# A rotation kernel: three output buffers and 63 chunks in place of two and 68, with the last load emitted later

## Chip, cores, metric

One core of a Trainium2 chip; the other cores are idle. The metric is the device time of the slowest core in microseconds (us), as the median of several runs. The span of a profile is about 1.8 us shorter than the time of the same run.

## The reference

`np.rot90(x, 1)` of an 8192 x 8192 float32 matrix: 268 MB are read and 268 MB written.

```python
def reference(x, k):            # k = 1
    return np.rot90(x, k)
```

## The kernel before

The matrix is worked through in macro tiles of 1024 rows x 4096 columns. The last one is cut into two of 512 rows, the "last macro tile but one" and the "last". Each macro tile has eight loads (2 MiB each, issued by SP, the sync engine, into an input buffer `a`), 64 chunks (DVE, the vector engine, copies 128 x 512 pieces with columns reversed into `ar`), and eight outputs. For an output, PE, the tensor engine, transposes 32 blocks into two tiles of PSUM, the memory that it writes to; ACT, the scalar engine, evicts (copies) each into an output buffer `ot`, and ACT issues the store (2 MiB). "The tail" is the work on the last two, smaller macro tiles. A load may be issued when all eight copies out of its buffer are done, and the buffer is that of the load two before. A store's buffer comes free when the store has landed.

```python
    a_pool = ctx.enter_context(tc.tile_pool(name="a_pool", bufs=2))
    r_pool = ctx.enter_context(tc.tile_pool(name="r_pool", bufs=68))
    o_pool = ctx.enter_context(tc.tile_pool(name="o_pool", bufs=2))
    psum_pool = ...                                   # bufs=2
    def load(r0, rt, c0):
        for t in range(rt):
            if loads < RT and loads % 4 >= 2:
                a = o_pool.tile([P, W], dt, tag="o")  # first eight loads only
            else:
                a = a_pool.tile([P, W], dt, tag="a")
            nc.sync.dma_start(out=a[:], in_=x[...])
            for j in range(W // CH):                  # 8 chunks a load
                ar = r_pool.tile([P, CH // P, P], dt, tag="ar")
                nc.vector.tensor_copy(out=ar[:], in_=a[...][:, :, ::-1])
                chunks[t, j] = ar
    def store(r0, rt, c0, chunks, end, first):
        for i, g0 in enumerate(range(0, W // P, G)):
            if end and (i + first) % 2 == 0:
                ot = a_pool.tile([P, F], dt, tag="a") # in the tail: input buffers too
            else:
                ot = o_pool.tile([P, F], dt, tag="o")
            for h in range(0, G, PW):
                pt = psum_pool.tile(...)
                for w in range(PW):
                    for t in range(rt):
                        nc.tensor.transpose(ps[...], chunks[t, ...][...], ident)
                nc.scalar.copy(o[...], ps)
                ...                                   # and, per output, the store:
                nc.scalar.dma_start(out=dst, in_=o[...])
    for m in most:
        store(*m, load(*m), False, 0)
    c1 = load(*before_last)
    c2 = load(*last)
    store(*before_last, c1, True, 1)
    store(*last, c2, True, 1)
```

Of the kernel before, what the change touches and what calls it, by code (L numbers as in the profile page):

```python
# [2 lines left out]

# [5 lines left out]

P = 128  # L10




R = 1024
RT = R // P
LAST = [4, 4]
W = 4096
CH = 512
F = 4096  # L20
FP = 2048


def whole_reads(nc):






    for fn in nc.m.functions:
        for block in fn.blocks:
            for n, ins in enumerate(block.instructions):
                if not isinstance(ins, mybir.InstDMACopy):
                    continue
                src = ins.ins[0]
                ap = [list(d) for d in src.ap]
                if len(ap) == 3 and ap[2][0] == 1 and ap[1][0] == ap[2][1]:
                    ap = [ap[0], [1, 1], [1, ap[1][1] * ap[2][1]]]
                    block.instructions[n] = copy.replace(  # L40
                        ins,
                        ins=[copy.replace(src, ap=ap)],
                        ant_dge_precooked=False,
                    )


def macro_tiles(N, M):

    tiles = [(r0, RT, c0) for r0 in range(0, N, R) for c0 in range(0, M, W)]
    r0, _, c0 = tiles.pop()  # L50
    for n in LAST:
        tiles.append((r0, n, c0))
        r0 += n * P
    return tiles


@with_exitstack
def kernel(
    ctx: ExitStack,
    tc: tile.TileContext,  # L60
    x: bass.AP,
    k: bass.AP,
    out: bass.AP,
):
    nc = tc.nc
    assert k == 1, f"only k=1 supported, got {k}"
    nc.at_finalize(whole_reads)

    N, M = x.shape
    dt = x.dtype  # L70

    consts = ctx.enter_context(tc.tile_pool(name="consts", bufs=1))
    ident = consts.tile([P, P], dt)
    make_identity(nc, ident)

    a_pool = ctx.enter_context(tc.tile_pool(name="a_pool", bufs=2))
    r_pool = ctx.enter_context(tc.tile_pool(name="r_pool", bufs=68))
    o_pool = ctx.enter_context(tc.tile_pool(name="o_pool", bufs=2))
    psum_pool = ctx.enter_context(
        tc.tile_pool(name="psum", bufs=2, space=bass.MemoryType.PSUM)  # L80
    )

    loads = 0

    def load(r0, rt, c0):





        nonlocal loads
        chunks = {}
        for t in range(rt):


            if loads < RT and loads % 4 >= 2:
                a = o_pool.tile([P, W], dt, tag="o")
            else:
                a = a_pool.tile([P, W], dt, tag="a")
            loads += 1  # L100
            nc.sync.dma_start(  # L101
                out=a[:], in_=x[r0 + t * P : r0 + (t + 1) * P, c0 : c0 + W]
            )
            for j in range(W // CH):
                ar = r_pool.tile([P, CH // P, P], dt, tag="ar")
                nc.vector.tensor_copy(  # L106
                    out=ar[:],
                    in_=a[:, j * CH : (j + 1) * CH].rearrange(
                        "r (b m) -> r b m", m=P
                    )[:, :, ::-1],  # L110
                )
                chunks[t, j] = ar
        return chunks

    def store(r0, rt, c0, chunks, end, first):





        rows = rt * P
        PW = 1
        while 2 * PW * rows <= FP:
            PW *= 2
        G = PW
        while 2 * G * rows <= F:
            G *= 2
        for i, g0 in enumerate(range(0, W // P, G)):
            if end and (i + first) % 2 == 0:
                ot = a_pool.tile([P, F], dt, tag="a")  # L130
            else:
                ot = o_pool.tile([P, F], dt, tag="o")
            o = ot[:, : G * rows].rearrange("m (g f) -> m g f", g=G)

            S = PW if end and r0 + rows == N and g0 + G == W // P else G
            for h in range(0, G, PW):
                pt = psum_pool.tile([P, FP], mybir.dt.float32, tag="ps")
                ps = pt[:, : PW * rows].rearrange("m (g f) -> m g f", g=PW)
                for w in range(PW):
                    g = g0 + h + w  # L140
                    for t in range(rt):
                        nc.tensor.transpose(  # L142
                            ps[:, PW - 1 - w, t * P : (t + 1) * P],
                            chunks[t, g * P // CH][:, g % (CH // P), :],
                            ident,
                        )
                nc.scalar.copy(o[:, G - PW - h : G - h, :], ps)  # L147

                done = h + PW
                if done % S == 0:  # L150
                    top = M - c0 - (g0 + done) * P
                    dst = out[top : top + S * P, r0 : r0 + rows].rearrange(
                        "(g m) f -> m g f", g=S
                    )
                    nc.scalar.dma_start(  # L155
                        out=dst, in_=o[:, G - done : G - done + S, :]
                    )

    tiles = macro_tiles(N, M)
    *most, before_last, last = tiles  # L160
    for m in most:
        store(*m, load(*m), False, 0)

    c1 = load(*before_last)
    c2 = load(*last)
    store(*before_last, c1, True, 1)
    store(*last, c2, True, 1)


# [1 line left out]
_INS = ['x', 'k']  # L171
_OUTS = [((8192, 8192), 'float32')]

_NUMBERS = {'k': 1}


# [26 lines left out]
```

## Time and profile before

Time before: 1269.7 us median (1269.53 to 1270.23). The page of the profile gives the busy times and the span in 40 slices. The DMA row is the mean busy share of the 16 DMA engines in tenths, the row below it what they moved. The last line here is the chain that ended last, by line.

```profile
span 1267.9 us, 10385 instructions
PE 708.5 (56%) x4096; PEld 668.7 (53%) x4096; DVE 355.1 (28%) x1024; ACT 467.6 (37%) x257; POOL 0.7 (0%) x6
...
DMA  9999999999999999999999999999999999999989
GB/s 399 418 430 429 430 429 429 430 428 430 428 429 429 429 428 429 429 430 429 428 430 429 429 427 425 424 429 429 429 429 423 417 426 427 428 429 429 429 361 374
...
q8 instruction: 32, 0.52, 0.2%
...
DMA out_dram<-ot 73%; ACT ot L147 19%; DMA a<-in_x_dram 4%; PE pt L142 1%; DVE ar L106 0%; ACTq L155 0%; SPq L101 0%; ACTq L147 0%; DVEq L106 0%
```

No compute engine is busy for more than 56%. The DMA row stands at 9 nearly throughout at about 429 GB/s. The Trainium skill ("Perfetto Trace Analysis", section Roofline) says that a single active core is bounded by its 16 DMA engines at about 435 GB/s together; the 429 of this trace agrees. The two weak slices at the end, 361 and 374, are what the change goes for. The windows of 5 us show them closer; the last two columns are the DMA share and GB/s.

```profile
core 0: us, PE busy (x) PEld busy (x) DVE busy (x) ACT busy (x) POOL busy (x), PEclk, DMA share, GB/s
1210.00:1215.00 5.00, 1.35 (x7) 1.36 (x8) 0.80 (x3) 3.27 (x2) 0.00 (x0) 0.87 0.83 349
1215.00:1220.00 5.00, 4.03 (x27) 3.78 (x25) 2.11 (x7) 0.56 (x2) 0.00 (x0) 0.79 0.82 347
1220.00:1225.00 5.00, 3.28 (x30) 3.24 (x31) 0.67 (x2) 4.25 (x3) 0.00 (x0) 1.00 0.43 180
1225.00:1230.00 5.00, 4.19 (x37) 3.67 (x34) 0.00 (x0) 4.33 (x3) 0.00 (x0) 1.00 1.00 416
1260.00:1265.00 5.00, 0.00 (x0) 0.00 (x0) 0.00 (x0) 0.00 (x0) 0.00 (x0) 0.50 0.94 388
```

Between 1210 and 1225 us the engines carry little: a hole worth 4.8 us of mean DMA time (the sum of (429 - rate)/429 x 5 us over the three windows). ACT's timeline shows where it comes from:

```profile
1205.54 0.55 ACTq L155 DMA_DIRECT2D out_dram<-ot  x1
1211.73 3.63 ACT L147 COPY ot<-pt 128x2048 f32<-128x2048 f32 x2 [6.22 <-DMA out_dram<-ot]
1215.39 0.55 ACTq L155 DMA_DIRECT2D out_dram<-ot  x1
1219.80 3.63 ACT L147 COPY ot<-pt 128x2048 f32<-128x2048 f32 x2 [4.44 <-DMA out_dram<-ot]
1223.47 0.55 ACTq L155 DMA_DIRECT2D out_dram<-ot  x1
```

With two output buffers, the eviction at 1219.80 waited (4.44 us idle) for the store issued at 1205.54. Its own store is issued only at 1223.47, when little is left in the queues.

Two more views are needed later: what SP's load issues waited for, and what the engines waited for in total (columns: total us, times, longest us).

```profile
SPq L101 <- DMA a<-in_x_dram: 798.5, 124, 12.3
SPq L101 <- DVE ar L106: 353.3, 124, 3.2
```

One view is not in the page: the 16 semaphore updates that each transfer leaves in the trace, one for each DMA engine. The Trainium skill ("DMA: Bandwidth & Descriptors", section "Why a DMA increments its semaphore by 16 and not by 1") says that the engines of one DMA finish independently and that only the full 16 means that the data has landed. The trace agrees: the 16 updates of the first load lie within 0.4 us, those of the load landing at 1217.8 spread over 8.9 us. "The slowest engine" below is the last of these 16; the kept records don't number the engines, so it need not be the same engine each time. There are 257 transfers (128 loads, 129 stores, the last output being two halves); the slowest engine's 247th lands at 1219.7, its last at 1267.0.

### The profile page before, as it was taken

How to read it: one execution, taken by the hardware profiler on the slowest of the kernel's cores; microseconds unless marked ns; L12 is line 12 of the kernel's file. 1: busy time of each engine (PE TensorE's matmuls, PEld its weight loads, DVE VectorE, ACT ScalarE, POOL GpSimd, SP SyncE). 2: the span in 40 equal slices, each digit the busy share in tenths (PEclk: the TensorE clock that was granted, in tenths of full speed). 3: DMA queues.
4: the chain of work that ended last, by engine and by line, in shares of the span. 5: the costliest groups of instructions: out<-in, count | busy, mean ns of one | idle time of the engine just before them, and what ended most of it. 6: DMA issues, size and time to landing. Idle time of an engine off the chain costs nothing.

```text
span 1267.9 us, 10385 instructions
## 1 busy us (share of the span) xinstructions
PE 708.5 (56%) x4096; PEld 668.7 (53%) x4096; DVE 355.1 (28%) x1024; ACT 467.6 (37%) x257; POOL 0.7 (0%) x6
## 2 busy tenths in 40 slices
PE   1456555655655556555556556565564655656674
PEld 0356455654655545554555545464564654645663
DVE  4422322232223322232223222232222322232210
ACT  0333344333433343333433334333433334333454
POOL 0000000000000000000000000000000000000000
PEclk9976767677677776776778767778777677677697
DMA  9999999999999999999999999999999999999989
GB/s 399 418 430 429 430 429 429 430 428 430 428 429 429 429 428 429 429 430 429 428 430 429 429 427 425 424 429 429 429 429 423 417 426 427 428 429 429 429 361 374
DMA packets 37057, 537.55 MB, mean 424 GB/s; under 512 B 4112, under 2 KB 4112, under 8 KB 4112
## 3 DMA queue, kind: packets, MB, share of 16 engines
q10 hardware_dynamic: 18576, 268.44, 49.9%
q1 hardware_dynamic: 18432, 268.44, 49.8%
q8 instruction: 32, 0.52, 0.2%
q14 instruction: 17, 0.14, 0.0%
HBM read 268.44 MB, written 268.44 MB: 423 GB/s over the span
## 4 chain that ended last, share of the span: by engine, by line
DMA 77%; ACT 19%; PE 1%; issue 1%; DVE 0%; ACTq 0%; SPq 0%; DVEq 0%
DMA out_dram<-ot 73%; ACT ot L147 19%; DMA a<-in_x_dram 4%; PE pt L142 1%; DVE ar L106 0%; ACTq L155 0%; SPq L101 0%; ACTq L147 0%; DVEq L106 0%
## 5 line engine op out<-in xcount | busy, mean ns | idle before, releaser
L142 PE MATMUL pt<-ident,ar 128*128 128x128 f32 x4096 | 708.5, 353 | 542.9 <-ACT ot L147 462.9
L142 PEld LDWEIGHTS pt<-ident,ar 128*128 128x128 f32 x4096 | 668.7, 189 | 582.4 <-ACT ot L147 493.5
L147 ACT COPY ot<-pt 128x2048 f32<-128x2048 f32 x256 | 466.3, 1869 | 745.1 <-DMA out_dram<-ot 732.6
L106 DVE COPY ar<-a 128x512 f32<-128x512 f32 x1024 | 355.1, 421 | 865.6 <-DMA a<-in_x_dram 781.4
L147 ACT ACT_TABLE_LOAD x1 | 1.3, 1283 | 41.0 <-DVE ar L106 41.0
masks.py:199 POOL TENSOR_SCALAR_AFFINE_SELECT ident<-ident 128x128 f32<-128x128 f32 x1 | 0.3, 294 | 0.1
masks.py:197 POOL MEMSET ident<- 128x128 f32 x1 | 0.2, 205 | 0.3 <-POOLq L184 0.3
L184 POOL MEMSET const-uint8-127<- 128x1 uint8 x1 | 0.1, 103 | 0.0
L184 POOL MEMSET const-bfloat16-1.0<- 128x1 bf16 x1 | 0.1, 102 | 0.0
L184 POOL MEMSET const-float32-0.0<- 128x1 f32 x1 | 0.1, 99 | 0.2 <-issue 0.2
L184 POOL MEMSET const-float32-1.0<- 128x1 f32 x1 | 0.1, 99 | 0.0
## 6 DMA issues: line engine op xcount, KB each, us to landing
a<-in_x_dram SPq DMA_DIRECT2D x128, 2048.0 KB, 16.8
out_dram<-ot ACTq DMA_DIRECT2D x127, 2048.0 KB, 15.8
out_dram<-ot ACTq DMA_DIRECT2D x2, 1024.0 KB, 12.9
```

The costliest lines, as they stand in the source:

```text
L106: nc.vector.tensor_copy(out=ar[:], in_=a[:, j * CH : (j + 1) * CH].rearrange("r (b m) -> r b m", m=P)[:, :, ::-1],)
L142: nc.tensor.transpose(ps[:, PW - 1 - w, t * P : (t + 1) * P], chunks[t, g * P // CH][:, g % (CH // P), :], ident,)
L147: nc.scalar.copy(o[:, G - PW - h : G - h, :], ps)
L184: nc = _bacc.Bacc("TRN2", target_bir_lowering=False, num_devices=1)
```

## The change

The intent: with a third output buffer, an output's eviction waits for the store three before instead of two before, so that in the tail stores are issued in time and the hole is filled. The space comes from the chunks, 63 instead of 68. That is one fewer than a macro tile has, and in the tail 32 + 32 chunks are loaded before an output frees any, so the last load must be emitted behind the first output, or the program would wait for itself.

```diff
-    r_pool = ctx.enter_context(tc.tile_pool(name="r_pool", bufs=68))
-    o_pool = ctx.enter_context(tc.tile_pool(name="o_pool", bufs=2))
+    r_pool = ctx.enter_context(tc.tile_pool(name="r_pool", bufs=63))
+    o_pool = ctx.enter_context(tc.tile_pool(name="o_pool", bufs=3))
...
-            if loads < RT and loads % 4 >= 2:
+            if loads < RT and loads % 5 >= 2:
...
-        return chunks
+            yield chunks
...
-            if end and (i + first) % 2 == 0:
+            if end and i % 2:
...
-    c1 = load(*before_last)
-    c2 = load(*last)
-    store(*before_last, c1, True, 1)
-    store(*last, c2, True, 1)
+    *_, chunks = load(*before_last)
+    outputs = store(*before_last, chunks, True)
+    rows = load(*last)
+    for _ in range(last[1] - 1):
+        next(rows)
+    next(outputs)
+    chunks = next(rows)
+    for _ in outputs:
+        pass
+    for _ in store(*last, chunks, True):
+        pass
```

No engine's order of instructions changes; only waits do.

## The prediction

> What bounds it. The page's slices show the DMA engines at 90% or more nearly throughout, at about 429 GB/s; PE is busy 56%, ACT 37%, DVE 28%. The chain of waits is 73% stores. 537 MB at 429.8 GB/s take 1251 us of the 1267.9 us span. The other 17 us, by windows of 20 us: 2.9 in the first 60 us, about 5 spread over the middle (dips near 740-820 and 960-1020), 9.1 after 1200 us, of which 2.9 is the final drain.
>
> The tail hole. Windows of 5 us: 349 GB/s at 1210-1215, 347 at 1215-1220, 180 at 1220-1225, then about 417 while only stores run. Against 429 that is 4.8 us. Its cause in the timeline: with two output buffers, output k's eviction waits for store k-2. The first output of the last macro tile but one waits until 1219.8 for the store issued at 1205.5, evicts for 3.6 us, and is stored from 1223.5, when the queue is all but dry. From then on ACT issues a store each 4.3 us, faster than the 4.9 to 5.0 us that 2 MiB take.
>
> What the change does. No transfer, copy, transpose or eviction is added or removed. Output k waits for store k-3. In the tail that first output can be evicted at about 1211.7 and stored from 1215.4, the next (into an input buffer, free at 1210.8) from 1219.7: both parts of the hole should be filled. The price: 63 chunks are one fewer than a macro tile's 64, so each tile's last copy waits for its first output's transposes (by the built program: the next load is issued about 6 us after the eighth lands, not 3). Loads take 16.8 us from issue to landing, so about 10 us of work still stand in the queues; I expect no cost. The last load's new place only prevents a deadlock: its own wait is unchanged, so it lands at 1218 as before. The start is equal within 0.6 us.
>
> How much is critical: not all 4.8 us. A DMA counts 16 engines that finish independently (the Trainium skill, "DMA: Bandwidth & Descriptors", section on why a DMA increments its semaphore by 16). The trace agrees: the 16 landings of one load spread over 0.4 us at the start, 8.9 us at 1217. The slowest engine lands at 1219.7, 1224.7, 1230.2 to 1230.8: it sat idle only 0.5 to 1.1 us in the hole, where the fast ones waited and all came level. Then one engine falls 1.9 us behind (a 16 KB instruction fetch at 1230.3) and sets the end, 1267.0. Without the hole the slowest engine goes on at 5.0 us a store: 1219.7 + 9 x 4.97 = 1264.5, or 1266.4 if a late fetch hits it. So the gain is 0.6 to 2.5 us, up to 4.8 if skew doesn't carry through. I predict 1267.3 us, range 1264.8 to 1269.7; faster by over 2% 0.01, within 2% 0.98, slower 0.01.
>
> Shown right by: no window after 1205 below 400 GB/s until the last 8 us; a ragged last slice, as fast engines finish first; landings of the last stores spread over 5 us or more, not 2; the last tile but one's first store issued about 1215. Shown wrong by: new dips at macro tile boundaries (DVE waiting for PE, loads issued late), or DMA share under 1 between 60 and 1200 us.
>
> What would make it wrong: the deeper store queue starving loads, so that each tile's first output waits (slower by a few us); or engine skew being reset elsewhere, giving the full 4.8 us.

## More of the kernel before

```profile
ACT ot L147 <- DMA out_dram<-ot: 732.6, 119, 7.0
...
ACT ot L147 <- PE pt L142: 11.6, 15, 3.4
```

Once its data had landed, no load issue waited longer than 3.2 us for DVE. ACT waits for stores, hardly ever for PE.

## The result

The change takes 1271.2 us (1270.82 to 1273.59, 4 runs), before 1269.72. It is 1.5 us slower where 0.6 to 2.5 us of gain were predicted, and outside of the predicted range. The ratio is 1.0015 with a 95% interval of 0.9998 to 1.0032. Ratios here are the mean time of one kernel's fast runs over that of the other's of the same rounds, so not quite the ratio of the medians quoted. The interval just includes 1, but no run of either kernel lies in the other's range, and in later rounds it was 1271.12 against 1270.09 again (below). The same lines of the page after:

```profile
GB/s 399 419 431 430 429 429 429 428 429 430 429 429 428 429 429 428 427 427 426 429 429 421 430 422 429 428 420 427 409 429 427 412 429 425 429 427 414 430 424 345
...
DMA a<-in_x_dram 52%; DMA out_dram<-ot 24%; DVE ar L106 7%; PE pt L142 7%; ACT ot L147 7%; ACTq L155 1%; DVEq L106 0%; ACTq L147 0%
```

The second to last slice has risen from 361 to 424. But slices further forward have fallen: 409 and 412, 414 near the 29th, 32nd and 37th. The chain that ended last is now mostly loads. The tail by windows, and ACT's timeline there:

```profile
1210.00:1215.00 5.00, 2.43 (x18) 2.19 (x16) 2.77 (x8) 0.09 (x1) 0.00 (x0) 0.91 0.99 423
1215.00:1220.00 5.00, 3.17 (x19) 3.17 (x20) 0.00 (x0) 3.86 (x3) 0.00 (x0) 0.78 1.03 434
1220.00:1225.00 5.00, 4.78 (x39) 4.55 (x38) 2.78 (x8) 3.64 (x3) 0.00 (x0) 0.88 1.00 423
1225.00:1230.00 5.00, 4.43 (x41) 4.15 (x40) 0.00 (x0) 3.79 (x3) 0.00 (x0) 1.00 1.00 413
1260.00:1265.00 5.00, 0.00 (x0) 0.00 (x0) 0.00 (x0) 0.00 (x0) 0.00 (x0) 0.50 0.77 320
```

```profile
1208.80 0.55 ACTq L155 DMA_DIRECT2D out_dram<-ot  x1
1214.91 3.64 ACT L147 COPY ot<-pt 128x2048 f32<-128x2048 f32 x2 [6.15 <-DMA out_dram<-ot]
1218.58 0.55 ACTq L155 DMA_DIRECT2D out_dram<-ot  x1
...
1224.15 0.55 ACTq L155 DMA_DIRECT2D out_dram<-ot  x1
```

The hole is gone: 423 to 434 GB/s where before had 349, 347 and 180, and the eviction at 1214.91 no longer leaves the queue dry. The last stores are ragged as predicted: their 16 landings spread over 5.1 us (before: 2.0), and the window 1260 to 1265 moves 320 GB/s, as the fast engines have finished. The slowest engine takes 44.8 us from its 247th transfer to the end, against 47.3 in before. That is a gain of 2.5 us, at the upper end of what was predicted.

But it reaches the 247th transfer at 1223.7 us instead of 1219.7. So 4.0 us were lost earlier, and 4.0 - 2.5 = 1.5 us is the result. The waits after:

```profile
SPq L101 <- DMA a<-in_x_dram: 773.4, 123, 11.5
SPq L101 <- DVE ar L106: 381.6, 123, 5.5
```

```profile
ACT ot L147 <- DMA out_dram<-ot: 481.5, 83, 7.1
...
ACT ot L147 <- PE pt L142: 268.5, 47, 18.6
```

Two things have changed. SP's longest wait for DVE is 5.5 us instead of 3.2. And ACT now waits 268.5 us for PE, up to 18.6 us at once: the stores run ahead within a macro tile, and its first output waits for the eighth load. One boundary between macro tiles, in before and after (timeline; start, duration, engine, instruction, and in brackets the idle time before it and who ended it):

```profile
1139.07 2.77 DVE L106 COPY ar<-a 128x512 f32<-128x512 f32 x8 [7.08 <-DMA a<-in_x_dram]
...
1141.87 10.22 SPq L101 DMA_DIRECT2D a<-in_x_dram  x2
...
1147.08 0.55 ACTq L155 DMA_DIRECT2D out_dram<-ot  x1
```

```profile
1142.06 2.44 DVE L106 COPY ar<-a 128x512 f32<-128x512 f32 x7 [7.00 <-DMA a<-in_x_dram]
...
1144.76 1.87 ACT L147 COPY ot<-pt 128x2048 f32<-128x2048 f32 x1 [14.97 <-PE pt L142]
1146.47 0.43 DVE L106 COPY ar<-a 128x512 f32<-128x512 f32 x1 [1.98 <-PE pt L142]
1146.93 8.04 SPq L101 DMA_DIRECT2D a<-in_x_dram  x2
...
1149.13 0.55 ACTq L155 DMA_DIRECT2D out_dram<-ot  x1
```

In before, the eight copies of the eighth load follow each other and the next load is issued 2.8 us after the first of them (1139.07 to 1141.87). In after, seven copies follow each other, the eighth waits 1.98 us for PE, and the load is issued 4.9 us after the first copy (1142.06 to 1146.93). ACT had idled for 14.97 us by then. The windows at this boundary, before and then after:

```profile
1145.00:1150.00 5.00, 4.07 (x33) 3.60 (x31) 1.04 (x4) 1.87 (x1) 0.00 (x0) 0.95 1.01 429
1150.00:1155.00 5.00, 0.42 (x2) 0.42 (x3) 1.74 (x6) 2.34 (x2) 0.00 (x0) 0.73 1.02 433
```

```profile
1145.00:1150.00 5.00, 4.79 (x39) 4.55 (x38) 0.43 (x1) 3.72 (x3) 0.00 (x0) 0.89 1.00 410
1150.00:1155.00 5.00, 4.43 (x41) 4.14 (x40) 2.78 (x8) 3.42 (x2) 0.00 (x0) 1.00 1.03 370
```

370 GB/s at a DMA share of 1.03: the engines are not idle, their packets take longer. (The share counts a packet's whole time in the window in which it starts, so it can pass 1.) In the trace's packet records, the 16 KiB load packets that started between 1152 and 1154 us took 0.98 us on average in after, where 0.61 us is usual.

So there were two candidates for the 4.0 us: stores that run ahead because of the third output buffer, and loads that come late because of the 63 chunks.

### The profile page after: what moved, and what is told of

The parts are those of the page before. It is cut to its first block, busy times and chain, and to the rows that moved or that the text cites. A ratio compares the mean times of both kernels' runs of the same rounds, so it can differ in the third digit from the quotient of the medians.

```text
span 1269.4 us, 10385 instructions
## 1 busy us (share of the span) xinstructions
PE 664.9 (52%) x4096; PEld 620.8 (49%) x4096; DVE 356.3 (28%) x1024; ACT 468.1 (37%) x257; POOL 0.7 (0%) x6
## 4 chain that ended last, share of the span: by engine, by line
DMA 76%; DVE 7%; PE 7%; ACT 7%; issue 1%; ACTq 1%; DVEq 0%
DMA a<-in_x_dram 52%; DMA out_dram<-ot 24%; DVE ar L106 7%; PE pt L142 7%; ACT ot L147 7%; ACTq L155 1%; DVEq L106 0%; ACTq L147 0%
## 5 line engine op out<-in xcount | busy, mean ns | idle before, releaser
L142 PE MATMUL pt<-ident,ar 128*128 128x128 f32 x4096 | 664.9, 337 | 585.1 <-ACT ot L147 369.7
L142 PEld LDWEIGHTS pt<-ident,ar 128*128 128x128 f32 x4096 | 620.8, 178 | 628.9 <-ACT ot L147 399.9
```

The source lines that it names most:

```text
L142: nc.tensor.transpose(ps[:, PW - 1 - w, t * P : (t + 1) * P], chunks[t, g * P // CH][:, g % (CH // P), :], ident,)
```

## The experiments

All gave the correct result. Each was timed in five rounds, with before in the same rounds at 1270.0 to 1270.1 us (the first two rows are the runs told of above). In the table, "interval" is the mean time between the issues of the first and the second load of a macro tile (14 tiles; the second waits for the copies of the tile before's eighth load); "load packet" is the mean duration of 16 KiB load packets between 60 and 1200 us; "247th" and "rest" are the slowest engine's landing of the 247th transfer and the time from there to its last. These four columns come from the one profiled execution of each kernel.

| kernel | output buffers, chunks | time (range), us | ratio to before (95%) | interval, us | load packet, ns | 247th, us | rest, us |
|---|---|---|---|---|---|---|---|
| before | 2, 68 | 1269.7 (1269.5 to 1270.2) | 1 | 9.9 | 614.6 | 1219.7 | 47.3 |
| the change | 3, 63 | 1271.2 (1270.8 to 1273.6) | 1.0015 (0.9998 to 1.0032) | 12.1 | 618.7 | 1223.7 | 44.8 |
| after_again | 3, 63 | 1271.1 (1270.8 to 1272.5) | 1.0010 (0.9998 to 1.0023) | 12.1 | 619.4 | 1224.1 | 44.8 |
| order_only | 2, 68 | 1270.0 (1269.5 to 1270.1) | 1.0000 (0.9987 to 1.0012) | 9.9 | 613.5 | 1219.4 | 47.7 |
| o2_c64 | 2, 64 | 1269.8 (1269.4 to 1270.2) | 1.0000 (0.9986 to 1.0013) | 9.9 | 613.6 | 1219.3 | 47.8 |
| o2_c63 | 2, 63 | 1273.6 (1272.9 to 1275.2) | 1.0031 (1.0018 to 1.0043) | 12.1 | 619.5 | 1223.9 | 47.5 |
| o2_c57 | 2, 57 | 1273.0 (1271.7 to 1275.0) | 1.0028 (1.0015 to 1.0041) | 13.1 | 621.1 | 1222.8 | 47.4 |
| third_tail | 2 (3 in the tail), 63 | 1272.2 (1270.2 to 1273.0) | 1.0013 (1.0001 to 1.0026) | 12.2 | 618.5 | 1222.5 | 44.9 |
| a3_c63 | 2 (3 input), 63 | 1269.3 (1269.1 to 1269.8) | 0.9996 (0.9984 to 1.0009) | 9.8 | 613.1 | 1218.9 | 47.9 |
| a3_first0 | 2 (3 input), 63 | 1268.0 (1267.6 to 1268.4) | 0.9985 (0.9973 to 0.9998) | 10.1 | 612.7 | 1219.9 | 45.2 |
| first0 | 2, 68 | 1268.3 (1267.7 to 1268.9) | 0.9987 (0.9973 to 1.0000) | 9.9 | 614.7 | 1220.0 | 46.1 |
| o2_c68_scratch | 2, 68 | 1269.9 (1269.3 to 1270.5) | 0.9999 (0.9986 to 1.0011) | 9.9 | 614.7 | 1219.8 | 47.3 |
| o3_c68 | 3, 68 | 1267.6 (1267.3 to 1268.0) | 0.9980 (0.9966 to 0.9994) | 9.9 | 613.1 | 1220.2 | 45.1 |
| o3_c63_tfirst | 3, 63 | 1266.8 (1266.4 to 1268.1) | 0.9975 (0.9963 to 0.9988) | 9.8 | 612.6 | 1219.1 | 44.8 |

In the first four, theory 1 blamed the third output buffer and theory 2 the missing chunk. I held theory 1 for the likelier.

### o2_c63: the chunks alone

```diff
 (of the change)
-    o_pool ... bufs=3        loads % 5 >= 2
+    o_pool ... bufs=2        loads % 4 >= 2
```

> Two output buffers as before, but 63 chunks and the last load behind the first output. Theory 1 (the third output buffer lets the stores run ahead, so that the store queue is empty at each macro tile's boundary and the engines lose about 4 us there by the tail): the boundaries are as in before, the tail hole of 4.8 us is back, 1269.7 us within 1. Theory 2 (63 chunks, fewer than the 64 of a tile, hold back the loads after a boundary): the dips at the boundaries stay, and with the tail hole back the time is 1272 to 1274 us.

Measured: 1273.6 us, slower than before by 0.31%, and slower than the change. The slowest engine's 247th transfer is at 1223.9 us, as in the change, with two output buffers. ACT hardly waited for PE (13.7 us in all), so no store ran ahead. Theory 1 falls: the 4 us are lost without the third buffer. Theory 2 fits.

### third_tail: the third buffer in the tail alone

```diff
 (of the change, with two o buffers and loads % 4)
+    x_pool = ctx.enter_context(tc.tile_pool(name="x_pool", bufs=1))
+            elif (r0, c0, i) in THIRD:       # last output of the last full macro tile,
+                ot = x_pool.tile(...)        # first output of the last macro tile
```

> 63 chunks and the new place of the last load as in the change, but the third output buffer is used for two outputs of the tail only; all outputs before rotate over two. Theory 1: no dips at the boundaries beyond those of before, no hole in the tail, the slowest engine runs from about 1220 us at 5 us a store to a last landing near 1264.5 (1266.5 if a late instruction fetch hits it): 1267 to 1269 us, faster than both kernels. Theory 2: dips as in the change, about 1271 us.

Measured: 1272.2 us, with a wide range. The tail is that of the change (44.9 us), the loss before it is there too (1222.5 in the profiled execution, which with 1270.2 us was the fastest of the five). My expectation of 1267 to 1269 was wrong for the same reason: the 63 chunks had stayed.

### order_only: the place of the last load alone

```diff
 (of the change)
-    r_pool ... bufs=63    o_pool ... bufs=3    loads % 5 >= 2
+    r_pool ... bufs=68    o_pool ... bufs=2    loads % 4 >= 2
```

> Before with its 68 chunks and two output buffers, only the last load emitted behind the first output of the last macro tile but one. Both theories: no engine's order changes and its own wait is the same, so 1269.7 us within 0.5 and the tail hole as in before. A rival that blames the place of the last load expects 1271 us.

Measured: 1269.96 us, as before. The new place of the load costs nothing and gains nothing.

### first0: the tail's rotation turned round, nothing else

```diff
 (of before)
-    store(*before_last, c1, True, 1)
-    store(*last, c2, True, 1)
+    store(*before_last, c1, True, 0)
+    store(*last, c2, True, 0)
```

> Before with only the rotation of the tail's buffers turned round: the first output of the last macro tile but one goes into the input buffer that is free at 1210.8 us, so its store is issued at about 1219.2 instead of 1223.5. Theory 1 with engine skew (the slowest engine, not the mean, sets the end): that is before the slowest engine runs dry at 1224.7, so it gains what it idled, 0.5 to 2.5 us: 1267.2 to 1269.3 us, though the mean rate still dips at 1210 to 1220. If the mean rate set the end, it would gain about 2.9 us (the later part of the hole): 1266.8.

Measured: 1268.25 us, 1.7 us faster than before by the medians, with an interval that reaches 1.0000. The windows of its tail:

```profile
1210.00:1215.00 5.00, 1.63 (x11) 1.39 (x10) 1.15 (x4) 2.94 (x2) 0.00 (x0) 0.82 0.85 359
1215.00:1220.00 5.00, 5.00 (x25) 5.00 (x24) 1.81 (x6) 2.56 (x2) 0.00 (x0) 0.50 0.73 308
1220.00:1225.00 5.00, 4.34 (x37) 3.86 (x36) 0.97 (x3) 3.66 (x3) 0.00 (x0) 1.00 0.67 282
```

The three windows sum to 949 GB/s x 5 us, where before has 876. By the mean rate this is only 73 x 5 / 429 = 0.9 us better. The store was issued at 1222.56, later than I expected, because the output's second half waited for PE. The slowest engine takes 46.1 us for the rest, 1.2 less than in before; profiled, both the mean and the slowest engine would give a gain of about 1 us. This run therefore doesn't tell them apart. It does show that a large part of the hole can stay open at a small price.

### o2_c64: one chunk more

```diff
-    r_pool ... bufs=68
+    r_pool ... bufs=64     (with order_only's other lines)
```

> Two output buffers and 64 chunks, exactly one macro tile. Theory 2, now sharpened (with fewer chunks than a tile's 64, the tile's last copy waits for transposes of the tile's own first output, so the second load after each boundary is issued about 12.0 us after the one before it instead of 9.8): at 64 the wait falls on outputs of the tile before, which are long done, so load intervals stay 9.8 us, and the time is that of before, 1270.0 us within 1. If instead each chunk less costs something, it lies between 1270 and 1273.6, near 1273.

Measured: 1269.8 us, interval 9.9 us, as with 68. From 68 to 64 chunks nothing happens; from 64 to 63 there are 3.8 us. It is not the number of chunks but the one wait that it brings: at 64 the last copy of a tile takes the space of a chunk of the tile before, which PE read long ago.

### o2_c57: more copies behind the wait

```diff
-    r_pool ... bufs=63
+    r_pool ... bufs=57     (of o2_c63)
```

> Two output buffers and 57 chunks: seven of the last load's eight copies come after the wait instead of one, so the second load after each boundary is issued about 6 x 0.35 = 2.1 us later still, an interval of about 14 us. Sharpened theory 2: the cost at the boundaries grows from 3.6 us to at least 6 us, 1276 us or more. If only the existence of a wait mattered: 1273.6.

Measured: 1273.0 us, the same as with 63, not 1276 or more. The interval came out as 13.1 us on average (10.8 to 14.7) and SP's longest wait for DVE as 7.2 us:

```profile
SPq L101 <- DVE ar L106: 466.2, 124, 7.2
```

So the cost does not grow with the lateness. The landings show a difference: the spread between the engines stays between 1 and 3 us for the whole run (medians of 24 transfers; from the 145th to the 240th transfer it is 4.4 us or more in all others). When the loss arises can't be read from the slowest engine here: its 49th transfer lands at 249.5 us, 2.7 later than in before, but its 121st at 600.9, level with before.

### a3_c63: the third buffer as an input buffer

```diff
 (of o2_c63)
-    a_pool ... bufs=2        loads % 4 >= 2
+    a_pool ... bufs=3        loads % 5 >= 3
```

> The third buffer goes to the inputs instead of the outputs, still 63 chunks. The last copy of a tile waits as in the change, but the load that waits for it is now the third one after it, with two loads still standing in the queue. If the late issue of the load is what costs: no cost at the boundaries, the slowest engine at the 247th transfer near 1220 us, the tail hole as in before: 1269.5 to 1270.5. If the lack of chunks costs in some other way (the first outputs wait, the slow load packets come from the copies): 1273 us as with two buffers.

Measured: 1269.3 us, interval 9.8, the 247th transfer at 1218.9. DVE still waits for PE, 797 us in all (84 in before), but a load no longer waits for the last copies of the load two before, and the cost is gone. So neither the lack of chunks as such nor DVE's wait costs anything here; what went with the cost is the late issue of the load.

### a3_first0: that, with the tail mended too

```diff
 (of a3_c63)
-            if end and i % 2:
+            if end and i % 2 == 0:
```

> As a3_c63, and the tail's outputs begin with an input buffer, which is free from about 1201 us on. If the late load is the cost and the slowest engine's idle time in the tail is the gain, both are mended: the slowest engine goes from 1220 us to the end in 44.9 us as in the change, last landing near 1264.8: 1267 to 1268 us, faster than before, the change and first0. If not: as a3_c63 or above.

Measured: 1268.0 us; rest 45.2 us. It beats before and the change, as expected, but is about level with first0.

### o2_c68_scratch and o3_c68: the cell that the change could not have

With three output buffers, there is no room for 64 chunks. 12288 bytes a partition were won from a scratch area that the framework reserves for a kind of transfer not used here.

```diff
 (o2_c68_scratch of before; o3_c68 of the change, with bufs=68 chunks)
-    nc = _bacc.Bacc("TRN2", target_bir_lowering=False, num_devices=1)
+    nc = _bacc.Bacc("TRN2", target_bir_lowering=False, num_devices=1, dynamic_dma_scratch_size=4096)
```

> Control: before with only the scratch area cut to 4096 bytes. Nothing uses it, and only addresses move: 1270.0 us within 0.4. Another time would mean that o3_c68 can't be read as three buffers alone.

Measured: 1269.92 us: the scratch area alone does nothing.

> The cell that the change could not have: three output buffers with before's 68 chunks. The space comes from the framework's DMA scratch area, cut from 16384 to 4096 bytes a partition, which this kernel's transfers do not use. If the third buffer's gain is the tail alone (2.4 us by the slowest engine) and all of the change's loss is the missing 64th chunk: load intervals 9.8 us at the boundaries, slowest engine at 1219.7 for the 247th transfer, 44.9 us more to the end, 1267.0 to 1267.8 us. If the third buffer itself costs at the boundaries: 1269 or above.

Measured: 1267.6 us, 0.20% faster than before. The 247th transfer is at 1220.2 us, the rest takes 45.1. Its waits, SP's and then ACT's:

```profile
SPq L101 <- DVE ar L106: 350.6, 123, 3.2
```

```profile
ACT ot L147 <- DMA out_dram<-ot: 494.2, 87, 7.1
ACT ot L147 <- PE pt L142: 248.9, 39, 19.0
```

SP's longest wait for DVE is back at 3.2 us. ACT still waits for PE for 248.9 us, 19.0 at the longest, as in the change. So the stores do run ahead with three buffers, and it costs nothing.

With this the four cells are there. Against before, by the medians of the same rounds: 63 chunks alone +3.6 us (1273.6 - 1270.0), the third buffer alone -2.5 (1267.6 - 1270.1), both +1.0 (1271.1 - 1270.1). The two effects add up: 3.6 - 2.5 = 1.1.

### o3_c63_tfirst: the change, with the wait made short

```diff
 (of the change)
-                for w in range(PW):
-                    g = g0 + h + w
-                    for t in range(rt):
+                for t in range(rt):
+                    for w in range(PW):
+                        g = g0 + h + w
                         nc.tensor.transpose(...)
```

> The change with the transposes of each PSUM tile in row-tile order, so that the 64th copy waits for the 18th transpose of the first output instead of the 25th. Theory 2: the second load after a boundary is issued some 1 to 1.7 us earlier than in the change (interval about 10.5 to 11 us instead of 12.0), and part or all of the 4 us comes back: 1267.5 to 1270 us. If the lateness within 2.2 us does not matter: 1271.2.

Measured: 1266.8 us, the fastest of all, 0.25% faster than before. One boundary:

```profile
1137.90 2.77 DVE L106 COPY ar<-a 128x512 f32<-128x512 f32 x8 [6.99 <-DMA a<-in_x_dram]
...
1138.38 5.59 PE L142 MATMUL pt<-ident,ar 128*128 128x128 f32 x34 [8.98 <-DVE ar L106]
...
1140.70 10.23 SPq L101 DMA_DIRECT2D a<-in_x_dram  x2
```

All eight copies run through, and the next load is issued 2.8 us after the first of them, as in before. It worked better than the transpose count alone had promised: in this order PE has most of the first half's transposes done before the eighth load lands, and only a few stand between its landing and the one that frees the chunk. The time is below the expected range, and why it is 0.8 us below o3_c68 wasn't tried. The interval is 9.8 us, the 247th transfer at 1219.1, the rest 44.8.

### after_again: the change in these rounds

> The change itself, unaltered, in the same rounds as the three others: about 1271.2 us, the slowest engine at about 1223.7 for the 247th transfer, load intervals of 12.0 us after each boundary.

Measured: 1271.1 us, 247th at 1224.1, rest 44.8: all as the first time.

## Why the prediction was wrong

- **What bounds the kernel, and the hole**: right. The tail hole was filled as described; its windows went from 180 to 349 up to 423 to 434 GB/s.
- **How much of the hole is critical**: right. Not 4.8 us: the slowest engine gained 2.5 us from the 247th transfer on, in the change and again in third_tail (2.4), o3_c68 (2.2) and o3_c63_tfirst. The landings show two parts. In before, two of the slowest engine's steps are longer than the usual 5.0 us: 6.1 in the hole (to 1230.8) and 6.2 right after it (to 1237.0), where one engine falls behind. In the change all steps are 4.9 to 5.0. The prediction had left open whether the second part would be gained, so that the upper end was reached is partly luck. The ragged end (spread 5.1 us) is as predicted.
- **The last load's new place**: right; order_only.
- **The step that failed** is the price of the 63 chunks: "the next load is issued about 6 us after the eighth lands, not 3 [...] so about 10 us of work still stand in the queues; I expect no cost." The wait itself was found and about rightly sized (the load is issued 5.1 us after the eighth has landed, 2.9 in before; means of 14 tiles). Its cost was not 0 but 3.6 us (o2_c63; 3.5 by after_again against o3_c68). o2_c64, a3_c63 and o3_c63_tfirst each take the lateness away in another way, and in each the cost is gone with it.
- **Why the reckoning failed**: the slack was mis-sized. The 16.8 us from issue to landing are 6.9 us until the load before has landed and 9.9 us for the load itself, and only the first part is slack; the prediction took the wait off the sum of both. At the late issue one earlier load is under way, and it lands on the slowest engine 4.8 us later (mean of 14 tiles; 6.9 in before), not 10, and on the engine furthest ahead 1.5 us later. For the slowest engine this figure is 6.9 us or more in all kernels without the loss; in those with it, it is 4.7 to 4.9, and 2.8 in o2_c57. An engine furthest ahead that runs out of loads is not the cost by itself: in before, over the last eight tiles, it had landed that load 1.5 us before the next one was issued, and nothing was lost.
- **The course of the loss**: up to the 145th transfer the change loses nothing (slowest engine at 718.9 us in both kernels) although the loads after each boundary are late from the third macro tile on; from there to the 247th it loses 4.0 us.
- **The rival that the prediction named**, stores that starve the loads: wrong. They do run ahead, and o3_c68 shows that this is free.
- **The predicted sign**: half right. Dips at the boundaries came, and loads were issued late. DMA share under 1 did not come: by windows of 20 us it is never under 0.99, and it is 1.03 at 370 GB/s.

What stays open: why a late load slows the packets. Load packets are slower in every kernel with late loads (618.5 to 621.1 ns on average, 612.6 to 614.7 in all others). With some 925 load packets for each engine in that stretch, 4.1 ns more are 3.8 us for an average engine in the change, about the size of the loss. The packet records also show where: of the load packets over 0.7 us (again between 60 and 1200 us), 234 of 275 in the change start while the second load of a macro tile, the late one, is the last that was issued; in before 11 of 138. Their excess over 0.61 us there adds up to 5.8 us for an average engine (before 0.3), elsewhere to 0.9 (before 2.7). So the loss is not idle time (over this stretch the DMA share is 1.006 in both kernels): packets around the late load are slow.

In the window of 0.98 us at 1152 us nearly all packets in flight are loads, but that alone is not the reason: in before, loads alone run from 3.5 to 30 us, at 0.61 us a packet. Why they are slow wasn't tried. Nor is it settled why 57 chunks cost no more than 63: its slow packets begin with the third macro tile and add up to more (7.3 us behind the late loads), and with a spread of 1 to 3 us they may hold back the fast engines rather than the slowest, but that is an argument from the landings alone.

## What to carry to other kernels

When buffers are moved from one pool to another, ask at which count the smaller pool begins to make a tile wait for itself: here 68 to 64 chunks were free, and the 64th was worth 3.6 us. Reckon the slack of a queue from when the work already in it will land (4.8 us here), not from a transfer's time from issue to landing (16.8), and gains at the end with the engine that is furthest behind. A DMA share of 1 does not show that a late transfer is free; compare GB/s and packet times too. A wait that can't be bought off with space can sometimes be shortened by order: transposing in the order in which the chunks are needed back made the change worth 3.3 us (1266.8 against 1270.1) with no byte more.

## What the Trainium skill lacked or had wrong

- "DMA: Bandwidth & Descriptors", section "Why a DMA increments its semaphore by 16 and not by 1": engines that "finish independently" is right, but nothing says how far apart they get. Here the 16 landings of a transfer drift from 0.4 us apart to as much as 9.7 in before and 11.6 in o3_c68. Filling a hole of 4.8 us by the mean rate gained the slowest engine 2.5 us at most.
- "Runtime: NRT & Kernel Launch", section "Instruction fetch mechanics", calls crossing a 16 KiB block "mostly hidden". It does not say what the fetch takes from the DMA engines. The profile counts 32 such packets, each of about 1 us on a DMA engine by the packet records. In a kernel bound by its DMA engines that may not be hidden: in before, the 16 landings of the store at 1230.8 us lie within 0.7 us, and in the next store, after the packet at 1230.3, one engine lies 1.9 us behind and stays there. That this packet is the cause is inferred from the time.
- "Perfetto Trace Analysis", section "Optimization Strategy", says that the same gap repeating on the engine that should be saturated can mean too little SBUF. That was so here, but there was no gap to see: the DMA share stayed at 1.0 (1.03 at 370 GB/s), and only GB/s and the duration of packets showed it.
- "DMA: Bandwidth & Descriptors", section Specifications, lists about 358 GB/s as the HBM limit of a core without saying in that row that it is the share with both cores of a pair active; this core, alone, moved 429 GB/s. "Perfetto Trace Analysis", section Roofline, says it.
- No page says that load packets can take 0.98 us instead of 0.61 for some microseconds after a load was issued late (at 1152 to 1154 us in the change); the cause is open.
